# A recurrent mixer's TensorE order written by a planner in the source, small matmuls in runs, and a norm factor moved behind the projection

## The chip, the core and the metric

The kernel runs on one NeuronCore of one Trainium2 chip. The metric is the device time of one execution in microseconds (us). Every engine of the core (TensorE, VectorE, ScalarE, GpSimd, and SyncE, whose queue issues most of the DMAs) works through its own instructions in order and waits on semaphores for the others. In the profile TensorE's matmuls are called PE and its weight loads PEld, VectorE is DVE, ScalarE is ACT, GpSimd is POOL, SyncE is SP.

## What is computed

A decoder trunk of two layers on a sequence of 1024 tokens of width 1024, float32. The first layer's mixer has eight retention heads and eight RWKV-7 heads side by side; the second layer's is a sliding-window attention. Each is followed by a SwiGLU feed-forward block (FFN). Cut to what the change touches:

```python
n = rms_norm(h, norm1_g[0])            # x * rsqrt(mean(x^2) + eps) * g
z = n @ w_in                           # 1024 x 3840: q,k,v,g of retention; r,k,v,w,a,g of RWKV
q = rotary(q); k = rotary(k) / 8
o = chunk_retention(q, k, v)           # chunks of 128, state carried from chunk to chunk
ret_out = head_group_norm(o) * silu(g)
zs = z_rwkv + mu * (token_shift(z_rwkv) - z_rwkv)
...                                    # decay, gate and removal key from small low-rank projections
y = rwkv7_scan(r, decay, k, v, -kk, kk * a)   # delta rule, one state of 64 x 64 for each head
rwkv_out = (head_group_norm(y) + bonus) * gate
h = h + concat(ret_out, rwkv_out) @ w_out
h = h + swiglu(rms_norm(h, norm2_g[0]))       # and so on: attention, a second FFN, a last norm
```

## The kernel before, in words

Everything is stored transposed: features on the 128 partitions, tokens along the free axis, in two halves of 512 tokens (`hf` 0 and 1). A weight is read as tiles of 128 output features by 1024 inputs. `wload` loads one (512 KB) through SP's queue into one of two raw buffers `wr`, ScalarE rounds it to fp32r (`wh`, L163), and GpSimd subtracts to get the rest (`wl`, L164). `gemm` (L172 to L174) then issues 24 fp32r matmuls of 128x512 for the tile: for each of the eight input blocks high by high, high by low, low by high, all into one PSUM tile `ps_f`, of which there are three. All other matmuls of the mixer are plain float32 and small; each stands in the trace as two records, a transpose as one.

`mixer0` handles one half after the other. `norm` loads the half's eight x tiles, squares them on ScalarE (L188), adds them on VectorE (L193), sums over the partitions with a matmul against a constant (L195), turns that into the factor r = rsqrt(mean + eps) (L197, L198), loads x again, multiplies x by gain and r (L208) and splits the product (L178, L180) into the normalised input `nT` of all projections. So no projection starts before the factor is known.

The heads are worked in pairs `p` = 0 to 3 (two heads fill 128 partitions), the pairs of RWKV in units of two pairs. For one pair `rw_proj` makes three projections through `shifted` (a `gemm`, a copy of PSUM to `z` by ScalarE at L338, the token shift), and `rw_a1` makes decays, keys and the tiles `AR`, `BK`, `UV` (with small matmuls at L380, L388, L397, L423 and transposes at L432). For a unit, `rw_a2` makes the 64x64 products inside chunks, `GG` (L476), with transposes and identity matmuls (L488, L494, L500). `rw_inv` inverts triangular 32x32 blocks on VectorE: `GG` goes to DRAM (`dn`) and back as `DT`, 31 steps of two instructions follow (L530, L534), and the result goes out (`dg`) and back as `GT`. `rw_w` combines the blocks (L557 to L604), `rw_chain` carries the state through eight chunks (matmul L625, VectorE L631, one after the other), and `rw_y` makes the output in the one PSUM tile `ps_y`: for each chunk and head a 64x64 matmul with the state (L648) and an accumulating one with 128 rows (L649) alternate. Norm, bonus and gate follow (L652 to L661), and the result goes to DRAM (`cats`).

`ret` does one retention pair: four projections with rotary parts on SP's DMA queue, transposes, scores (L760: four chunks of one head, then four of the other), the state, and the output, in which a 128-row matmul with a block-diagonal state tile `Sb` (L772) and two others (L774) alternate into one PSUM tile. After both halves, `wout` multiplies the concatenated outputs with `w_out` (eight `gemm`s for each half; its addition on VectorE is L321), and the FFN follows.

The program is written with a tile framework. It allocates the buffers, places the semaphores, and its scheduler decides the order of each engine's instructions ahead of time from its own estimates. In the kernel before, that order is what TensorE runs: the scheduler mixes single matmuls of the projections with small matmuls, one by one. TensorE then takes them in that order, whatever is late.

Of the kernel before, what the change touches and what calls it, by code (L numbers as in the profile page):

```python
# [101 lines left out]

class Kern:
    def __init__(self, ctx, tc, A, out):
# [3 lines left out]
        self.ps = ctx.enter_context(tc.tile_pool(name="ps", bufs=1, space=bass.MemoryType.PSUM))  # L108
# [9 lines left out]
        self.cats = [self.dram(f"cat{hf}", [KT, P, HT]) for hf in range(2)]  # L118

# [19 lines left out]

    def s8(self, pool, tag, n, dt=F32):  # L140

        return [self.t(pool, [P, 4, HT], tag, n, dt) for _ in range(n)]

    def pst(self, tag, shape):
        return self.t(self.ps, shape, "ps_" + tag, {"f": 3, "m": 2, "r": 1, "c": 1, "y": 1}[tag])
# [6 lines left out]
    def wload(self, ap, width=1024):  # L152

        nc = self.nc
        raw = self.t(self.pp, [P, 1024], "wr", 2)
        nc.sync.dma_start(raw[:, :width], ap)
# [9 lines left out]
        return res  # L166

# [33 lines left out]
    def norm(self, h, g, s8):  # L201

# [3 lines left out]
        for k in range(KT):  # L206
            n = self.t(self.pp, [P, HT], "nq", 4)
            nc.vector.scalar_tensor_tensor(  # L208
                out=n, in0=h(k), scalar=self.col(g, k), in1=r, op0=ALU.mult, op1=ALU.mult
            )  # L210
            a, b = s8[k // 4][:, k % 4, :], s8[2 + k // 4][:, k % 4, :]
            self.split(n, a, b, k % 2 == 0)
            res.append((a, b))
# [15 lines left out]
    def mixer0(self):  # L229
# [25 lines left out]
        self.wa, self.gl, self.nT, self.cs = [None, None], [None, None], [None, None], [None, None]  # L255
        proj, st = {}, {}

        def pj(hf, p):
            proj[hf, p] = self.rw_proj(hf, p)

        def a1(hf, p):
            st[hf, p] = self.rw_a1(hf, p, proj.pop((hf, p)))

        def unit(hf, pairs):
            ss = [st.pop((hf, p)) for p in pairs]
            for p, x in zip(pairs, ss):
                self.rw_a2(x)
            self.rw_inv(ss)
            for x in ss:
                self.rw_w(x)  # L270
            self.rw_chain(hf, pairs, ss)
            for p, x in zip(pairs, ss):
                self.rw_y(hf, p, x)

        for hf in range(2):

            def x(k):
                t = self.t(self.pp, [P, HT], "nq", 4)
                nc.sync.dma_start(t, self.A["xT"][k, :, hf * HT : (hf + 1) * HT])
                return t  # L280

            self.nT[hf] = self.norm(x, "n1a", self.s8(self.pp, "s8", 4, F32R))
            self.ropes(hf)
            self.lora(hf)
            pj(hf, 0)
            a1(hf, 0)
            pj(hf, 1)
            a1(hf, 1)
            unit(hf, (0, 1))
            self.ret(hf, 0)  # L290
            pj(hf, 2)
            a1(hf, 2)
            self.ret(hf, 1)
            pj(hf, 3)
            a1(hf, 3)
            unit(hf, (2, 3))
            self.ret(hf, 2)
            self.ret(hf, 3)
        gr.__exit__(None, None, None)
        self.ghx, self.hx = self.pool("hx", "left")  # L300
        self.h[0] = self.wout(0, self.s8(self.pp, "s8", 4, F32R), self.s8(self.hx, "h0", 2))
        gm.__exit__(None, None, None)

    def wout(self, hf, ch8, h8):

        nc = self.nc
        hi, lo = ch8[0:2], ch8[2:4]
        ch = []
        for k in range(KT):
            c = self.t(self.pp, [P, HT], "nq", 4)  # L310
            nc.sync.dma_start(c, self.cats[hf][k])
            a, b = hi[k // 4][:, k % 4, :], lo[k // 4][:, k % 4, :]
# [11 lines left out]
    def ropes(self, hf):  # L324
        self.cs[hf] = (
            self.const(self.rp, "cos", (hf * HT, HT), eng=self.nc.sync),
            self.const(self.rp, "sin", (hf * HT, HT), eng=self.nc.sync),
        )

    def shifted(self, hf, ti, out):  # L330

        nc = self.nc
        w = self.wload(self.A["w_in"][16 + ti])
        ps = self.pst("f", [P, HT])
        self.gemm(ps, w, self.nT[hf])
        z = self.t(self.rp, [P, HT + 1], "z", 1)
        nc.gpsimd.tensor_copy(z[:, 0:1], self.zlast[:, ti : ti + 1])
        nc.scalar.copy(z[:, 1 : HT + 1], ps)  # L338
        nc.gpsimd.tensor_copy(self.zlast[:, ti : ti + 1], z[:, HT : HT + 1])
        nc.gpsimd.tensor_tensor(out=out, in0=z[:, 0:HT], in1=z[:, 1 : HT + 1], op=ALU.subtract)  # L340
        nc.vector.scalar_tensor_tensor(
            out=out, in0=out, scalar=self.col("mu", ti), in1=z[:, 1 : HT + 1], op0=ALU.mult, op1=ALU.add
        )

    def lora(self, hf):
        nc = self.nc
        wa = self.wa[hf] = self.t(self.mp, [P, HT], "wa", 1)
        gl = self.gl[hf] = self.t(self.mp, [P, HT], "gl", 2)
        self.shifted(hf, 12, wa)
        nc.scalar.activation(wa[0:64, :], wa[0:64, :], AF.Tanh)  # L350
        self.shifted(hf, 13, gl)
        nc.scalar.activation(gl, gl, AF.Tanh, scale=0.5)
        nc.vector.tensor_scalar(out=gl, in0=gl, scalar1=0.5, scalar2=0.5, op0=ALU.mult, op1=ALU.add)

    def rw_proj(self, hf, p):
        r = self.t(self.mp, [P, HT], "rr", 1)
        k = self.t(self.mp, [P, HT], "rkk", 1)
# [711 lines left out]
```

## Time and profile before

| | us |
|---|---|
| median of three runs | 2885.43 (2883.05 to 2896.56) |
| the profiled execution, whole | 2885.72 |
| its span, first to last instruction | 2883.9 |
| first matmul of a projection starts | 38.3 |
| last output of the RWKV heads is finished (end of L661, start of the last one 867.1) | 868 |
| last addition of the output projection (L321) starts | 965.4 |
| TensorE busy over the span | 2626.0 (91%) |
| VectorE, ScalarE, GpSimd busy | 1038.0, 1019.7, 1314.8 |

The change lies in the first 966 us. A busy time is the time in which at least one such instruction was under way, so divided by the count it gives the spacing of records that follow one another closely, while the mean duration of one includes its way through the array. A row of the waits says which instruction TensorE stood before, and what came last of that which it waited for. The granted clock is the share of full speed that the throttle let TensorE have.

### The profile page before, as it was taken

Reading aid. Unit: us, or ns where it says so; the run is one execution under the profiler, and the core shown is the slowest. Engines: PE = TensorE matmul, PEld = TensorE weight load, DVE = VectorE, ACT = ScalarE, POOL = GpSimd, SP = SyncE. Lnnn points to the kernel's source line nnn. Section 1 sums busy time; section 2 is a strip of 40 time slices with the busy share of each in tenths; the row PEclk is TensorE's granted clock in tenths of the full one; section 3 lists DMA queues with packets and bytes.
Section 4 is the critical chain, followed back from the end, with each engine's and each line's share of the span. In section 5 each row is a group of like instructions: output and inputs, shape, how many; then the busy total and the mean of one; then the engine's idle time right before and its main releaser. Section 6 shows DMA issues by size and latency. Waiting matters only on the chain. (4 is left out here: it accounts for less than half of the span.)

```text
span 2883.9 us, 35835 instructions
## 1 busy us (share of the span) xinstructions
PE 2626.0 (91%) x13484; PEld 2049.2 (71%) x13484; DVE 1038.0 (36%) x1810; ACT 1019.7 (35%) x1865; POOL 1314.8 (46%) x1140
## 2 busy tenths in 40 slices
PE   4799987888898899998999999989999999899997
PEld 2576664666676778886867888867678888688876
DVE  2554553554652421123193111333831112511113
ACT  3424323424343432223353222344533223422223
POOL 3533323433434555554424555544145555555553
PEclk9898998998998999998999999999999999999999
DMA  4221222121224222323302232432022223322332
GB/s 132 91 69 46 68 63 90 55 69 43 69 78 152 68 95 93 96 95 118 116 30 74 95 95 89 131 112 78 29 77 95 91 89 105 102 95 92 95 98 81
DMA packets 122908, 249.64 MB, mean 87 GB/s; under 512 B 37744, under 2 KB 48624, under 8 KB 122736
## 3 DMA queue, kind: packets, MB, share of 16 engines
q1 hardware_dynamic: 116480, 237.68, 25.8%
q10 hardware_dynamic: 6256, 9.67, 1.0%
q8 instruction: 107, 1.75, 0.2%
q14 instruction: 65, 0.53, 0.1%
HBM read 227.25 MB, written 14.68 MB: 84 GB/s over the span
## 5 line engine op out<-in xcount | busy, mean ns | idle before, releaser
L164 POOL TENSOR_TENSOR wl<-wr,wh 128x512 fp32r<-128x512 f32 (+1 forms) x776 | 997.1, 1287 | 1223.0 <-ACT wh L163 1146.0
L172 PE MATMUL ps_f<-s,wh 128*128 128x512 f32 x2336 | 939.6, 404 | 37.5 <-ACT s L178 27.2
L173 PE MATMUL ps_f<-s,wh 128*128 128x512 f32 x2336 | 938.9, 402 | 15.3 <-POOL s L180 12.0
L174 PE MATMUL ps_f<-s,wl 128*128 128x512 f32 x2336 | 940.9, 403 | 2.1 <-POOL wl L164 2.1
L163 ACT CAST wh<-wr 128x512 fp32r<-128x512 f32 (+1 forms) x776 | 472.3, 611 | 1316.3 <-PE ps_f L173 1086.8
L172 PEld LDWEIGHTS ps_f<-s,wh 128*128 128x128 f32 x2336 | 449.9, 193 | 152.8 <-ACT s L178 33.9
L173 PEld LDWEIGHTS ps_f<-s,wh 128*128 128x128 f32 x2336 | 449.5, 192 | 124.1 <-POOL s L180 17.8
L174 PEld LDWEIGHTS ps_f<-s,wl 128*128 128x128 f32 x2336 | 450.7, 193 | 107.4 <-issue 10.1
L173 PE MATMUL ps_f<-hl,wh 128*128 128x512 f32 x704 | 278.7, 396 | 18.8 <-POOL hl L180 18.8
L172 PE MATMUL ps_f<-hh,wh 128*128 128x512 f32 x704 | 275.7, 393 | 9.3 <-DVE h L819 7.4
L174 PE MATMUL ps_f<-hh,wl 128*128 128x512 f32 x704 | 274.5, 392 | 0.0
L819 DVE SCALAR_TENSOR_TENSOR h<-ps_f,h 128x512 f32<-128x512 f32 x192 | 132.5, 690 | 341.8 <-PE ps_f L174 341.8
L802 DVE SCALAR_TENSOR_TENSOR sl<-sl,ps_f 128x512 f32<-128x512 f32 x88 | 60.4, 687 | 437.2 <-ACT sl L801 437.2
L173 PEld LDWEIGHTS ps_f<-hl,wh 128*128 128x128 f32 x704 | 133.1, 189 | 55.4 <-POOL hl L180 28.5
L806 DVE TENSOR_TENSOR sl<-sl,ps_f 128x512 f32<-128x512 f32 x88 | 60.5, 687 | 289.0 <-PE ps_f L174 288.9
L172 PEld LDWEIGHTS ps_f<-hh,wh 128*128 128x128 f32 x704 | 133.0, 189 | 40.1 <-ACT nq L188 7.8
L174 PEld LDWEIGHTS ps_f<-hh,wl 128*128 128x128 f32 x704 | 133.1, 189 | 27.2 <-issue 0.2
L180 POOL TENSOR_TENSOR hl<-sl,hh 128x512 fp32r<-128x512 f32 x88 | 113.9, 1295 | 20.4 <-ACT hh L178 20.4
L180 POOL TENSOR_TENSOR s<-nq,s 128x512 fp32r<-128x512 f32 x40 | 63.8, 1604 | 77.5 <-ACT s L178 77.5
L193 DVE TENSOR_TENSOR nq<-nq,nq 128x512 f32<-128x512 f32 x70 | 59.8, 854 | 44.1 <-ACT nq L188 41.7
L178 ACT CAST s<-nq 128x512 fp32r<-128x512 f32 x80 | 48.3, 618 | 64.0 <-DVE nq L208 51.4
L909 ACT ACTIVATE s<-s,st 128x256 f32<-128x256 f32 (+1 forms) x128 | 62.0, 486 | 18.4 <-DVE st L906 18.4
(224 smaller groups left out, 2299.8 us busy)
## 6 DMA issues: line engine op xcount, KB each, us to landing
wr<-in_w_gate SPq DMA_DIRECT2D x88, 512.0 KB, 3.2
wr<-in_w_up SPq DMA_DIRECT2D x88, 512.0 KB, 3.3
wr<-in_w_down SPq DMA_DIRECT2D x128, 256.0 KB, 2.6
wr<-in_w_in SPq DMA_DIRECT2D x60, 512.0 KB, 3.3
wr<-in_w_down SPq DMA_DIRECT2D x64, 192.0 KB, 2.3
wr<-in_w_qkv SPq DMA_DIRECT2D x24, 512.0 KB, 3.2
nq<-in_xT SPq DMA_DIRECT2D x32, 256.0 KB, 2.7
wr<-in_w_out SPq DMA_DIRECT2D x16, 512.0 KB, 3.2
```

The costliest lines, as they stand in the source:

```text
L163: nc.scalar.copy(hi[:, :n], raw[:, c])
L164: nc.gpsimd.tensor_tensor(out=lo[:, :n], in0=raw[:, c], in1=hi.bitcast(F32)[:, :n], op=ALU.subtract)
L172: nc.tensor.matmul(ps, hi, rh, start=k == 0, stop=False)
L173: nc.tensor.matmul(ps, hi, rl, start=False, stop=False)
L174: nc.tensor.matmul(ps, lo, rh, start=False, stop=k == n - 1)
L178: nc.scalar.copy(hi, src)
L180: e.tensor_tensor(out=lo, in0=src, in1=hi.bitcast(F32), op=ALU.subtract)
L193: nc.vector.tensor_tensor(out=acc, in0=acc, in1=sq, op=ALU.add)
L802: V.scalar_tensor_tensor(out=sl, in0=sl, scalar=1.0, in1=pg, op0=ALU.add, op1=ALU.mult)
L806: V.tensor_tensor(out=sl, in0=sl, in1=pu, op=ALU.mult)
L819: V.scalar_tensor_tensor(out=hk, in0=ps, scalar=0.5, in1=hk, op0=ALU.mult, op1=ALU.add)
L909: S.activation(s[:, h, kw], s[:, h, kw], AF.Exp, bias=m[:, h : h + 1], accum_out=den[:, h : h + 1])
```

## The change

Three things change in the first mixer. First, TensorE's order is written out when the program is built: the parts of the mixer are generators that yield what they need next and how long to wait for it, and a class `Plan` runs them against an estimated clock `now`, which each matmul advances by an estimate. Whenever no generator is due, `Plan.step` issues the next three matmuls of the current projection. Each matmul is passed to `keep_in_program_order`, so that the framework's scheduler no longer moves it on TensorE; the other engines are scheduled as before. The projections are jobs in one fixed list. The units are chained: from the second one on, a unit's pair makes `GG` only after the unit ahead has made its output (`y{u-1}`), while its keys and decays are made earlier, for which `rr`, `rkk`, `rv`, `BK` get two buffers and `AR` four.

Second, small matmuls are regrouped: those of `GG` and of the retention scores alternate between the two heads (upper and lower 64 rows) with two PSUM tiles, and the two parts of an output that alternated in one PSUM tile are now made one after the other in two PSUM tiles, which ScalarE and VectorE add. `Sb` is gone: the state part uses two 64-row matmuls.

Third, `nT` is x times the gain alone (`gained`); the factor r is multiplied into the projections' results when they leave PSUM: on VectorE for RWKV, v and g (in place of ScalarE's copies), and through cos and sin for q and k. The first half's x is loaded once and its squares are summed by eight matmuls between those of the first projection; the second half's squares are summed on GpSimd while the first half is worked.

The `s8` tiles of four blocks become `n8` tiles of two blocks, in the whole kernel, and the first mixer has its own PSUM pool (three `f`, four `m`, one `c`).

```diff
+class Plan:
+    def step(self):
+        c = self.cur
+        if c is None:
+            if not self.jobs:
+                return None
+            t = self.time(self.jobs[0]["need"], 0.0)
+            if t is None or t > self.now:
+                return t
+            self.prefetch()
+            c = self.cur = self.jobs.popleft()
+            self.prefetch()
+            c["ps"], c["k"], c["rhs"] = self.K.pst("f", [P, HT]), 0, c["rhs"]()
+        ...
+        (hi, lo), (rh, rl) = c["hl"][k], c["rhs"][k]
+        self.K.mm(c["ps"], hi, rh, start=k == 0, stop=False)
+        self.K.mm(c["ps"], hi, rl, start=False, stop=False)
+        self.K.mm(c["ps"], lo, rh, start=False, stop=k == n - 1)
+        ...
+    def run(self):
+        while self.gens or self.jobs or self.cur:
+            nxt = []
+            for g in self.gens:
+                t = self.time(g[1], g[2])
+                if t is not None and t <= self.now:
+                    try:
+                        need, d = next(g[0])
+                        g[1], g[2] = need, self.now + d
+                    except StopIteration:
+                        self.gens.remove(g)
+                    break
+                ...
+            else:
+                t = self.step()
+                ...
+    def mm(self, out, lhsT, rhs, **kw):
+        i = self.nc.tensor.matmul(out, lhsT, rhs, **kw)
+        self.tc.keep_in_program_order(i)
+        ...
+        if rhs.dtype == F32R:
+            self.plan.now += 0.000443 * n
+        else:
+            self.plan.now += max(0.05, 0.00167 * n * (0.6 if lhsT.shape[0] <= 64 or lhsT.shape[1] <= 64 else 1.0))
 def mixer0(self):
+        pl.chain(self.first_norm(x0))
+        for u, (hf, p0) in enumerate(units):
+            pl.chain(self.unit(u, hf, (p0, p0 + 1)))
+        for u, (hf, p0) in enumerate(units):
+            for p in (p0, p0 + 1):
+                pl.chain(self.pair(u, hf, p))
+        for hf in range(2):
+            for p in range(4):
+                pl.chain(self.ret(hf, p))
+        pl.chain(self.second_norm())
+        self.lora(0)
+        jobs(0, "rkv", (0, 1))
+        jobs(0, "ret", (0, 1))
+        jobs(0, "rkv", (2, 3))
+        jobs(0, "ret", (2, 3))
+        self.lora(1)
+        jobs(1, "rkv", (0, 1))
+        jobs(1, "ret", (0,))
+        jobs(1, "rkv", (2, 3))
+        jobs(1, "ret", (1, 2, 3))
+        pl.run()
+    def gained(self, x, g, n8, k):
+        self.nc.scalar.activation(a, x, AF.Copy, scale=gc)
+        self.nc.vector.scalar_tensor_tensor(
+            out=b, in0=x, scalar=gc, in1=a.bitcast(F32), op0=ALU.mult, op1=ALU.subtract
+        )
+    def first_norm(self, x0):
+        for k in range(KT):
+            self.nT.append(self.gained(x0[k], "n1a", n8, k))
+            nc.scalar.activation(sq, x0[k], AF.Square)
+            ...
+            self.mm(ps, self.cst["ones"], sq, start=k == 0, stop=k == KT - 1)
 shifted:
-        nc.scalar.copy(z[:, 1 : HT + 1], ps)
+            nc.vector.tensor_tensor(out=z[:, 1 : HT + 1], in0=ps, in1=self.rs, op=ALU.mult)
 pair (was rw_a1 and rw_a2):
+        yield (), 6.0        # after the two low-rank matmuls
+        ...
+        yield ((f"r{hf}_{p}", 5.0), (f"v{hf}_{p}", 5.0)), 8.0
+        ...
+        yield (), 12.0
+        if u:
+            yield ((f"y{u - 1}", 1.0),), 0.0
+        for h in range(2):
+            pss = [self.pst("m", [P, 4, P]) for _ in range(2)]
+            for i in range(4):
+                for e in range(2):
+                    self.mm(pss[e][:, i, :], BK[half[e], c, ...], AR[half[e], c, :], start=True, stop=True)
 unit (was rw_inv, rw_w, rw_chain and rw_y):
+        yield tuple((f"n{u}_{p}", 3.5) for p in pairs), 0.0
+        ...                  # DT loads, then 31 steps, after each second one:
+            if j % 2:
+                yield (), 2.4
+        ...                  # dg stored, GT loaded
+        yield tuple((f"a{u}_{p}", 1.0) for p in pairs), 7.0
+        ...
+        for c in range(NCH): # the state
+            ...
+            yield (), 1.3
+            y1, y2 = self.pst("m", [P, NCH, 64]), self.pst("m", [P, NCH, 64])
+            for c in range(NCH):
+                for e, a in enumerate(half):
+                    self.mm(y1[a, c, :], UV[:, c, e, :], GG[:, c, e, 64:P], start=True, stop=True)
+            for c in range(NCH):
+                for a in half:
+                    self.mm(y2[a, c, :], GT[a, c, :], AR[a, c, 64:P], start=True, stop=True)
+            S.copy(y, y1.rearrange("p c t -> p (c t)"))
+            V.tensor_tensor(out=y, in0=y2.rearrange("p c t -> p (c t)"), in1=y, op=ALU.add)
 ret:
+            for e, a in enumerate(half):
+                self.mm(pss[e][:, c, :], k[a, tk], q[a, tk], start=True, stop=True)
+        ...
+        for c in range(4):
+            for e, a in enumerate(half):
+                self.mm(p1[a, c, :], vt[:, c, e, :], sc[e][:, c, :], start=True, stop=True)
+        for c in range(4):
+            for a in half:
+                self.mm(p2[a, c, :], Sc[a, c, :], qd[a, c, :], start=True, stop=True)
```

## The prediction

> **What bounds the kernel now.** I read the page first, then busy time and granted clock by stretch, TensorE's waits in the mixer, and its groups of small matmuls.
>
> ```profile
> span 2883.9 us, 35835 instructions
> PE 2626.0 (91%) x13484; PEld 2049.2 (71%) x13484; DVE 1038.0 (36%) x1810; ACT 1019.7 (35%) x1865; POOL 1314.8 (46%) x1140
> ```
>
> ```profile
> core 0: us, PE busy (x) PEld busy (x) DVE busy (x) ACT busy (x) POOL busy (x), PEclk, DMA share, GB/s
> 0.00:38.30 38.30, 2.11 (x3) 0.54 (x3) 7.04 (x13) 12.89 (x18) 7.50 (x16) 1.00 0.55 172
> 38.30:867.00 828.70, 716.30 (x5048) 528.05 (x5048) 433.25 (x791) 300.28 (x489) 323.77 (x356) 0.89 0.22 68
> 867.00:966.00 99.00, 88.90 (x373) 70.88 (x372) 23.27 (x31) 31.47 (x51) 43.68 (x34) 0.90 0.40 137
> 1031.00:2883.00 1852.00, 1764.57 (x7853) 1408.32 (x7852) 535.35 (x935) 639.08 (x1251) 896.68 (x707) 0.98 0.28 91
> ```
>
> TensorE bounds everything after 1031 us. The first 966 us are another matter: its busy time is 2.1 + 716.3 + 88.9 = 807.3, so it stands idle for 158.7 us: 36.2 before the first projection, 112.4 in the mixer, 10.1 in the output projection. VectorE is busy for 433 of 829 us there, so no other engine is the limit; what is lost is waits, slow small matmuls and clock. The change touches nothing after 966 us but the size of buffers, which I cost at nothing: the same matmuls at 95% busy cover it.
>
> ```profile
> engine line waited for: us in total, times, longest us
> PE ps_m L423 <- DVE rr L421: 40.4, 8, 6.7
> PE ps_m L195 <- DVE nq L193: 32.0, 1, 32.0
> PE ps_m L397 <- ACT rt L395: 20.2, 5, 7.5
> PE ps_f L172 <- ACT s L178: 11.6, 2, 7.4
> PE ps_c L563 <- DVE TZ L557: 8.1, 3, 3.4
> ```
>
> ```profile
> 0.00:867.00 867.00, 76.09 (x496) 53.02 (x496) 6.01 (x8) 4.78 (x8) 0.90 0.24 73
> ...
> 0.00:867.00 867.00, 413.25 (x1478) 289.15 (x1478) 5.43 (x8) 34.76 (x60) 0.90 0.24 73
> ...
> 1100.00:1300.00 200.00, 197.65 (x870) 162.64 (x869) 35.88 (x52) 6.51 (x11) 1.00 0.30 96
> ...
> 432.00:504.00 72.00, 53.26 (x193) 35.38 (x192) 25.20 (x26) 28.38 (x42) 27.13 (x31) 0.81 0.27 90
> ```
>
> The first row is `ps_y` alone: 153 ns a record. The second is `ps_f`: a projection's matmul takes 279.6 ns in the mixer, against 227.2 ns in the FFN (third row, at full clock). The fourth is a stretch of the mixer with 19 us of idle TensorE and a clock of 0.81.
>
> **The change part by part.** I sum the first 966 us, TensorE's busy time first.
>
> ```profile
> L476 PE MATMUL ps_m<-AR,BK 64*128 64x128 f32 x256 | 29.7, 284 | 0.7 <-DVE GG L480 0.2
> L760 PE MATMUL ps_r<-r,r 64*128 64x128 f32 x128 | 25.8, 356 | 6.7 <-DVE Sret L744 6.3 <-DVE r L762 0.3
> L625 PE MATMUL ps_c<-S,M 64*64 64x64 f32 x240 | 15.8, 229 | 0.0
> L595 PE MATMUL ps_m<-GG,W 64*64 64x128 f32 x256 | 15.7, 272 | 0.0
> L774 PE MATMUL ps_r<-r,r 128*64 128x128 f32 x112 | 13.1, 314 | 0.0
> L772 PE MATMUL ps_r<-r,r 128*128 128x128 f32 x50 | 12.9, 344 | 0.6 <-DVE r L762 0.6
> L604 PE MATMUL ps_m<-UV,GG 128*64 128x64 f32 x256 | 9.2, 225 | 0.5 <-DVE AR L600 0.3
> L494 PE MATMUL ps_m<-c_ident,AR 64*64 64x64 f32 x256 | 9.2, 221 | 0.0
> L782 PE MATMUL ps_m<-r,c_blk 128*128 128x512 f32 x16 | 8.7, 625 | 0.7 <-ACT r L780 0.7
> ```
>
> RWKV output. `y1` is 256 records of exactly L604's form, `y2` 256 of L494's, both in runs: 9.2 + 9.2 = 18.4 for 76.1, so -57.7. At L625's price `y2` is 16.9 and the gain 50.
>
> `GG`. In L476 four matmuls in a row use the same 64 rows, 116 ns a record. Now the halves alternate, as in L595 (61 ns, also 128 tokens): 15.7 for 29.7, -14.0. If two outputs of 128 columns don't overlap: 0. I take L595, the nearest row with alternating halves.
>
> Scores. 128 records at 61 ns are 7.8 for 25.8: -18.0; at L476's price, 14.8: -11.0.
>
> Retention output. L772 and L774, whole, are 12.9 x 56/50 + 13.1 x 128/112 = 29.4 (the window cuts the last pair). The new 256 records are 64-wide over 128 tokens, in runs: 15.7, so -13.7; at worst 0.
>
> Norm. Nine sums of squares for two, each 8.7/8 = 1.09: +7.6.
>
> Projections. The surplus is 1478 x (279.6 - 227.2) = 77 us. Part of it is splitting: a change of tile form costs 153 - 36 = 117 ns by the `ps_y` row. In the built order of instructions the tile form changes 510 times up to the last RWKV output before and 302 times after; 219 of the 510 are `ps_y`'s own, so elsewhere it is 291 against 302. Some 291 x 0.117 = 34 us stay; the other 43 are clock. I take -25, because the longest waits go, with 0 and -77 as ends.
>
> On this splitting the Trainium skill ("TensorEngine Tiling", Key Properties) says that changing the tiling mode, not just the tile, drains TensorE. The 153 against 36 ns agree with it, and it speaks against issuing projections in threes between small runs: by it alone the projections gain nothing.
>
> Busy: 807.3 - 57.7 - 14.0 - 18.0 - 13.7 + 7.6 - 25 = 686.5. Ends: 754 (gains of 50, 0, 11, 0, 0) and 634.
>
> Now idle time.
>
> ```profile
> wr<-in_w_in SPq DMA_DIRECT2D x60, 512.0 KB, 3.3
> nq<-in_xT SPq DMA_DIRECT2D x32, 256.0 KB, 2.7
> L163 ACT CAST wh<-wr 128x512 fp32r<-128x512 f32 (+1 forms) x776 | 472.3, 611 | 1316.3 <-PE ps_f L173 1086.8
> L164 POOL TENSOR_TENSOR wl<-wr,wh 128x512 fp32r<-128x512 f32 (+1 forms) x776 | 997.1, 1287 | 1223.0 <-ACT wh L163 1146.0
> ```
>
> Start. The first projection needs no factor. SP's queue holds eight x tiles ahead of the first weight: 8 x 0.26 + 0.52 = 2.6 MB, at the 172 GB/s of the first row 15 us, and 0.6 + 1.3 for the split with its hand-overs make 18 instead of 36. Eight x loads fewer in all; at a DMA share of 0.22 the rest of the DMAs are covered by compute.
>
> Long waits. The matmul of L397 was ordered too close behind ScalarE, that of L423 too close behind VectorE. The plan puts 6.0 us ahead of the first and at least 8.0 + 12.0 ahead of the second: -60.6. Late next is the inverse:
>
> ```profile
> L476 PE MATMUL ps_m<-AR,BK x64: 271/272/374, 333.7 to 344.9; 64*128 64x128 f32 x64
> L530 DVE TENSOR_TENSOR xt<-X,DT x31: 181/272/1378, 353.1 to 382.5; 128x126 f32<-128x126 f32 x3, 128x30 f32<-128x30 f32 x2, 128x56 f32<-128x56 f32 x2, 128x78 f32<-128x78 f32 x2
> L557 DVE STREAM_TRANSPOSE TZ<-GT x4: 432/434/436, 388.8 to 393.2; 32x256 f32<-32x256 f32 x4
> L625 PE MATMUL ps_c<-S,M x56: 216/218/267, 402.6 to 417.7; 64*64 64x64 f32 x56
> ```
>
> This is unit two. The 31 steps take 382.5 - 353.1 = 29.4 us, the plan allows 15 x 2.4 = 36; from the last step to L557 6.3, the plan 7.0. Only the state's step is tight: 15.1/7 = 2.16 us here, with output matmuls between, against 1.3 and its own matmuls (0.25) in the plan: up to 32 x 0.6 = 19 us, which I leave to the range, since those output matmuls (8 x 0.153 a step) explain it. For new waits at the fixed places I take 15; ends 0, and 61 + 19, as much as goes.
>
> Idle: 18 + (112.4 - 60.6) + 15 + 10 = 95.
>
> VectorE. 44 results leave PSUM there instead of through ScalarE:
>
> ```profile
> L424 DVE TENSOR_TENSOR bv<-rv,ps_m 128x512 f32<-128x512 f32 x8 | 5.5, 685 | 7.4 <-PE ps_m L423 7.4
> L338 ACT COPY z<-ps_f 128x512 f32<-128x512 f32 x28 | 16.3, 581 | 19.5 <-DVE rr L341 11.9 <-DVE rkk L341 3.8 <-PE ps_f L174 3.2
> L208 DVE SCALAR_TENSOR_TENSOR nq<-nq,pv,nq 128x512 f32<-128x512 f32 x15 | 14.3, 956 | 20.2 <-DMA nq<-in_xT 16.6 <-ACT nq L198 3.3
> ```
>
> With 16 sums of two PSUM tiles that is 60 x 0.685 = 41 us; `gained` and L208 cancel (16 of each), and the squares' sums leave. 433 becomes about 460, some 60% of the shorter stretch: costed at nothing, covered by TensorE. GpSimd takes seven sums and four products with cos and sin, about 15 us on 324, off the path.
>
> Sum: 686.5 + 95 = 781.5 for 966.0, so -184.5. The profiled execution took 2885.7 (span 2883.9 and 1.8 around it), 0.3 above the median of the runs: 2885.7 - 184.5 = 2701, forecast 2700. With the ends: 634 + 80 (no new wait) gives 2634; 754 + 160 gives 2834.
>
> **The rivals.** Waits change places. Order fixed on TensorE means that whatever is late on VectorE stops everything behind it, and the order before was static too and had 158.7 us of waits. Idle as before: +64, 2765. Against it: the plan's leads are longer than the rows above.
>
> The drain decides: the clock doesn't recover, the projections stay at 279.6 ns: +25, 2725.
>
> The clock recovers wholly: 227.2 ns, 2648. For it: 0.81 goes with 19 us idle, 1.00 with 2. The Trainium skill ("TensorE: Matmul & The Clock Gate", Part 1) says that an idle window of about 3.4 us halves the clock until a busy window has passed; the trace's stretches agree.
>
> Slower: the units' latency becomes the bound.
>
> ```profile
> L476 PE MATMUL ps_m<-AR,BK x256: 271/272/374, 145.2 to 763.1; 64*128 64x128 f32 x128
> ```
>
> Each unit now waits for the output of the one ahead, and VectorE, with the PSUM results in its queue, does the inverse between them. From L476 to the end of L625 is 84 us above, so about 90 with the output. Unit one's `GG` starts at about 125 (145.2 before, less 18): 125 + 4 x 90 + 70 for the last output projection is 555, hidden under 781. It shows from (781 - 195)/4 = 147 us a unit and makes the kernel slower from 193, 2.1 times what is measured; at 205 it is 2935. What could do it is SP's queue: weight loads stand behind the store `dg` that waits for the inverse, and two buffers cover 2 x 24 x 0.227 = 11 us.
>
> **How the numbers follow.** Forecast about 2700 (2665 to 2715): 0.42. Clock recovers, 2648: 0.16. Drain decides, 2725: 0.16. Waits change places, 2765, up to 2834 with its ends: 0.15. Slower: 0.08. The planned order brings nothing: 0.03. The range 2615 to 2825 leaves out the last two and the far ends. 0.5% (14 us) is about what can be told from no change; faster 0.89, same 0.03, slower 0.08.
>
> **What would show it.** Right: `y1` and `y2` at about 40 ns a record; `GG` near 60; the first projection near 18 us; the wait before the matmuls of `rr` and `rt` with `c_blk` gone; `ps_f` at 240 to 270 ns; output projection done near 780. Wrong: TensorE waiting for the state's steps, for GT, or for weight splits over many us in each unit, or VectorE over 80% busy in the mixer.

## The result, and the profile after

The changed kernel takes 2738.95 us (median; 2735.00 to 2743.06) where the kernel before takes 2885.33 (2883.05 to 2896.56): 0.9485 of the time, with a 95% interval of 0.9456 to 0.9515. The forecast was 2700, its range 2615 to 2825. The direction and the place were right, 146 us went where 185 were forecast, and one term of the sum is the chief reason.

The page of the changed kernel begins so (span, then busy time, share of the span and instructions of each engine):

```profile
span 2741.2 us, 36080 instructions
PE 2539.6 (93%) x13602; PEld 1983.9 (72%) x13602; DVE 1046.2 (38%) x1846; ACT 1017.0 (37%) x1861; POOL 1315.1 (48%) x1125
```

Busy time and granted clock of the changed kernel by stretch; `a:b`, its length, then busy us and instructions of each engine, the clock, the DMA share and GB/s:

```profile
core 0: us, PE busy (x) PEld busy (x) DVE busy (x) ACT busy (x) POOL busy (x), PEclk, DMA share, GB/s
0.00:827.10 827.10, 722.17 (x5540) 536.46 (x5540) 472.14 (x870) 342.64 (x554) 373.95 (x390) 0.92 0.30 90
0.00:16.70 16.70, 2.09 (x3) 0.52 (x3) 1.07 (x4) 3.21 (x5) 2.74 (x14) 1.00 0.88 279
16.70:766.00 749.30, 658.99 (x5271) 485.97 (x5272) 450.06 (x842) 318.14 (x514) 334.22 (x349) 0.91 0.28 80
766.00:827.10 61.10, 61.10 (x269) 49.97 (x267) 21.02 (x25) 21.28 (x36) 36.99 (x28) 1.00 0.47 158
888.00:2740.00 1852.00, 1764.79 (x7858) 1407.64 (x7858) 536.13 (x936) 639.53 (x1252) 899.30 (x708) 0.98 0.29 91
```

The output projection ends at 827 us instead of 966, and that is nearly the whole gain: the profiled executions differ by 2885.7 - 2743.1 = 142.6, the stretch by 139. The last 1852 us are the same to 0.3 us of TensorE. In the stretch TensorE's busy time fell from 807.3 to 722.2, its idle time from 158.7 to 827.1 - 722.2 = 104.9. VectorE is busy for 450 of 749 us of the mixer, 60%.

TensorE's longest waits in the first 850 us of the changed kernel (total, times, longest):

```profile
engine line waited for: us in total, times, longest us
PE ps_m L209 <- ACT nq L452: 14.1, 2, 13.2
PE ps_m L220 <- DVE r L883: 13.8, 3, 8.3
PE ps_m L220 <- DVE GG L631: 9.0, 1, 9.0
PE ps_c L209 <- DVE GT L821: 8.4, 3, 3.9
PE ps_f L209 <- POOL wl L278: 8.3, 5, 2.0
PE ps_f L209 <- ACT wh L277: 8.1, 5, 3.6
```

Before, two lines held 40.4 and 20.2 us and the start 32.0; now no line holds more than 14.1, and most rows of the whole list are one or two events. The first is still the start: 13.2 of its 14.1 us lie before TensorE's first matmul. `L883` is v's result leaving VectorE ahead of v's transposes, `L631` the mask on `GG`, `L821` the state's step.

The groups of small matmuls that the change regrouped, in the changed kernel (busy us and mean ns of one, then idle time before them; `L209` is the helper through which every matmul goes):

```profile
L209 PE MATMUL ps_m<-AR,BK 64*128 64x128 f32 x256 | 23.6, 315 | 5.8 <-DVE rt L856 3.8 <-ACT rt L850 1.3 <-DVE bv L616 0.4
...
L209 PE MATMUL ps_m<-nq,c_ones 128*128 128x512 f32 x18 | 12.0, 754 | 14.1 <-ACT nq L452 14.1
...
L209 PE MATMUL ps_m<-r,r 128*64 128x128 f32 x128 | 11.2, 316 | 1.4 <-DVE r L939 1.4
...
L209 PE MATMUL ps_m<-r,Sc 64*64 64x128 f32 x128 | 10.4, 301 | 0.0
...
L209 PE MATMUL ps_m<-wa,wua 64*128 64x512 f32 x32 | 10.1, 640 | 0.7 <-DVE UV L784 0.7
...
L209 PE MATMUL ps_m<-r,r 64*128 64x128 f32 x128 | 9.3, 283 | 3.8 <-issue 3.8
L209 PE MATMUL ps_m<-GG,UV 128*64 128x64 f32 x256 | 9.2, 225 | 0.0
L209 PE MATMUL ps_m<-AR,GT 64*64 64x64 f32 x256 | 9.2, 221 | 0.0
```

The last two rows are the RWKV output, 18.4 us in place of 76.1. `AR,BK` is `GG` (29.7 before), `r,r 64*128` the scores (25.8), `r,r 128*64` with `r,Sc` the retention output. The low-rank matmuls `wa,wua` took 9.0 and 8.9 us in two groups before, which is 17.9, and now 10.1.

The projections of the whole stretch (the tile `ps_f` alone), first before, then after:

```profile
0.00:966.00 966.00, 496.38 (x1824) 356.46 (x1824) 16.20 (x24) 34.76 (x60) 0.90 0.25 79
```

```profile
0.00:827.10 827.10, 492.45 (x1824) 350.69 (x1824) 41.09 (x60) 9.25 (x16) 0.92 0.30 90
```

The same 1824 records, and only 3.9 us less.

### The profile page after: what moved, and what is told of

Read it like the earlier page. It is cut to its first block, busy times and chain, and to the rows that moved or that the text cites. A ratio compares the mean times of both kernels' runs of the same rounds, so it can differ in the third digit from the quotient of the medians.

```text
span 2741.2 us, 36080 instructions
## 1 busy us (share of the span) xinstructions
PE 2539.6 (93%) x13602; PEld 1983.9 (72%) x13602; DVE 1046.2 (38%) x1846; ACT 1017.0 (37%) x1861; POOL 1315.1 (48%) x1125
## 5 line engine op out<-in xcount | busy, mean ns | idle before, releaser
L290 PE MATMUL ps_f<-n,wh 128*128 128x512 f32 x1856 | 734.0, 396 | 15.7 <-ACT n L296 15.7
L291 PE MATMUL ps_f<-n,wh 128*128 128x512 f32 x1856 | 734.4, 396 | 4.5 <-POOL n L298 2.8
L292 PE MATMUL ps_f<-n,wl 128*128 128x512 f32 x1856 | 732.4, 395 | 0.5 <-POOL wl L278 0.4
L290 PEld LDWEIGHTS ps_f<-n,wh 128*128 128x128 f32 x1856 | 352.2, 190 | 97.6 <-ACT n L296 19.1
L291 PEld LDWEIGHTS ps_f<-n,wh 128*128 128x128 f32 x1856 | 352.3, 190 | 85.8 <-issue 5.6
L292 PEld LDWEIGHTS ps_f<-n,wl 128*128 128x128 f32 x1856 | 352.3, 190 | 80.2 <-issue 6.0
L209 PE MATMUL ps_f<-n,wh 128*128 128x512 f32 x960 | 335.6, 432 | 11.0 <-ACT wh L277 8.1
L209 PEld LDWEIGHTS ps_f<-n,wh 128*128 128x128 f32 x960 | 182.9, 200 | 69.8 <-issue 17.1
L1001 DVE SCALAR_TENSOR_TENSOR sl<-sl,ps_f 128x512 f32<-128x512 f32 x88 | 60.4, 687 | 437.1 <-ACT sl L1000 437.1
L209 PE MATMUL ps_f<-n,wl 128*128 128x512 f32 x480 | 198.5, 414 | 8.5 <-POOL wl L278 8.3
L1005 DVE TENSOR_TENSOR sl<-sl,ps_f 128x512 f32<-128x512 f32 x88 | 60.4, 686 | 287.9 <-PE ps_f L292 287.8
L209 PEld LDWEIGHTS ps_f<-n,wl 128*128 128x128 f32 x480 | 96.1, 200 | 33.6 <-POOL wl L278 11.8
```

The costliest lines, as they stand in the source:

```text
L209: i = self.nc.tensor.matmul(out, lhsT, rhs, **kw)
L290: nc.tensor.matmul(ps, hi, rh, start=k == 0, stop=False)
L291: nc.tensor.matmul(ps, hi, rl, start=False, stop=False)
L292: nc.tensor.matmul(ps, lo, rh, start=False, stop=k == n - 1)
L1001: V.scalar_tensor_tensor(out=sl, in0=sl, scalar=1.0, in1=pg, op0=ALU.add, op1=ALU.mult)
L1005: V.tensor_tensor(out=sl, in0=sl, in1=pu, op=ALU.mult)
```

## The experiments

Three questions were open after the first look. How much is the regrouping and how much the order? What holds the projections at 270 ns a record (492.45 us for 1824; 272 before, 227.2 in the FFN), the pieces in which they are issued or the clock? And are the remaining waits worth anything? Every run is compared with the kernel before on the same chip. "End" is the end of the output projection, "idle" is that end less TensorE's busy time, and "half" is the time up to that end in which the trace's records of the granted clock say 0.50, added up.

| run | us | of before, 95% interval | end | idle | half |
|---|---|---|---|---|---|
| before | 2885.33 | 1 | 966 | 159 | 195 |
| after | 2738.95 | 0.9485 (0.9456 to 0.9515) | 827 | 105 | 130 |
| e1 scheduler's order | 2726.14 | 0.9443 (0.9413 to 0.9472) | 811 | 90 | 109 |
| e2 RWKV output alternates | 2815.93 | 0.9757 (0.9723 to 0.9792) | 900 | 104 | 198 |
| e3 leads halved | 2769.94 | 0.9601 (0.9570 to 0.9632) | 854 | 139 | 133 |
| e4 leads times 1.25 | 2732.17 | 0.9467 (0.9439 to 0.9495) | 819 | 104 | 109 |
| e5 heads in turn | 2732.38 | 0.9460 (0.9438 to 0.9483) | 817 | 90 | 106 |
| e6 start held back | 2724.98 | 0.9440 (0.9412 to 0.9467) | 806 | 95 | 106 |
| e7 no leads, scheduler alone | 2839.17 | 0.9831 (0.9807 to 0.9855) | 928 | 191 | 212 |
| e8 before, output in runs | 2826.50 | 0.9785 (0.9757 to 0.9812) | 905 | 161 | 137 |
| e9 six leads lengthened | 2720.12 | 0.9417 (0.9397 to 0.9438) | 805 | 100 | 85 |
| e10 e9 + e1 + e6 | 2711.39 | 0.9386 (0.9361 to 0.9411) | 794 | 93 | 68 |
| e11 e8 with two tiles | 2827.40 | 0.9793 (0.9767 to 0.9819) | 909 | 162 | 140 |
| e12 pieces of 12 | 2720.08 | 0.9418 (0.9397 to 0.9439) | 803 | 104 | 85 |

**The RWKV output alone, put back and taken alone.** In e2 the changed kernel's two kinds of output matmuls alternate one by one again, still into two tiles:

```diff
             for c in range(NCH):
                 for e, a in enumerate(half):
+                    self.mm(y2[a, c, :], GT[a, c, :], AR[a, c, 64:P], start=True, stop=True)
                     self.mm(y1[a, c, :], UV[:, c, e, :], GG[:, c, e, 64:P], start=True, stop=True)
-            for c in range(NCH):
-                for a in half:
-                    self.mm(y2[a, c, :], GT[a, c, :], AR[a, c, 64:P], start=True, stop=True)
```

> The changed kernel, but in the RWKV output the 64-row and 128-row matmuls alternate again, one by one, still into two PSUM tiles and at the same place of the plan. If each change of tile form costs the 117 ns read from the kernel before and TensorE's time bounds this stretch: the 512 records take about 78 us instead of 18, and the time is 2785 to 2800. Rival, that the runs lie in time in which TensorE would wait anyway: 2739 to 2755.

It took 2815.93 us, 77 more than the changed kernel and 16 more than I expected at most. The stretch and the two groups in e2:

```profile
core 0: us, PE busy (x) PEld busy (x) DVE busy (x) ACT busy (x) POOL busy (x), PEclk, DMA share, GB/s
0.00:900.10 900.10, 796.54 (x5540) 584.57 (x5540) 472.59 (x870) 344.46 (x554) 371.79 (x390) 0.89 0.27 83
```

```profile
L209 PE MATMUL ps_m<-GG,UV 128*64 128x64 f32 x256 | 55.7, 316 | 0.0
L209 PE MATMUL ps_m<-AR,GT 64*64 64x64 f32 x256 | 55.4, 312 | 0.0
```

The same 5540 records keep TensorE busy for 74 us longer (796.5 against 722.2; the two groups overlap), idle time is as it was, and the half-clock time rises from 130 to 198 us. By the trace's records the two groups together are under way for 93 us, and 76 of these lie at half clock.

In e8 the kernel before makes its output in two runs, 128-row matmuls first and 64-row ones behind, in its one tile; the counts and shapes are those of before, but the RWKV output of e8 is not the reference's (the tile seems not to keep the sum of both parts), so e8 counts for its time alone. In e11 the two runs go to two tiles, which ScalarE and VectorE add:

```diff
-        yps = self.pst("y", [P, HT])
+        y1, y2 = self.pst("y", [P, HT]), self.pst("c", [P, HT])
+        c0 = 1 if hf == 0 else 0
...
-                if not first:
-                    nc.tensor.matmul(yps[a, tk], St[a, c, :], AR[a, c, 64:P], start=True, stop=False)
-                nc.tensor.matmul(yps[a, tk], UV[:, c, e, :], GG[:, c, e, 64:P], start=first, stop=True)
+                nc.tensor.matmul(y1[a, tk], UV[:, c, e, :], GG[:, c, e, 64:P], start=True, stop=True)
+        for c in range(c0, NCH):
+            tk = slice(64 * c, 64 * c + 64)
+            for a in half:
+                nc.tensor.matmul(y2[a, tk], St[a, c, :], AR[a, c, 64:P], start=True, stop=True)
+        yy = self.t(mp, [P, HT], "rt", 6)
+        S.copy(yy, y1)
+        V.tensor_tensor(out=yy[:, 64 * c0 :], in0=y2[:, 64 * c0 :], in1=yy[:, 64 * c0 :], op=ALU.add)
```

> The kernel before with one edit: in the RWKV output the 128-row matmuls of all chunks come first and the 64-row ones after them, into the same PSUM tile. If the alternation alone, with the clock that it holds down, is worth 77 us: 2805 to 2830. Rival, that in this kernel the alternating matmuls lie in time in which TensorE waits for the chunk states anyway: 2860 to 2885.

> The kernel before, its RWKV output made in two runs into two PSUM tiles (the second is the one of the state's steps), added by ScalarE and VectorE as in the changed kernel. If the alternation of tile forms is worth as much here as where it was put back: 2805 to 2830, as with one PSUM tile. Rival, that the shared PSUM tile and eight more additions on VectorE eat it: 2850 to 2885.

They took 2826.50 and 2827.40 us, 60 us less than the kernel before each time. The stretch in e11:

```profile
core 0: us, PE busy (x) PEld busy (x) DVE busy (x) ACT busy (x) POOL busy (x), PEclk, DMA share, GB/s
0.00:909.00 909.00, 746.93 (x5422) 560.12 (x5422) 469.64 (x842) 349.34 (x566) 376.21 (x405) 0.92 0.28 84
```

Busy time falls by 60.4 (807.3 to 746.9) and idle time stays (159 before, 162 here). So this one regrouping, some twenty lines, is 60 of the 146 us when done alone and 77 when taken out of the rest. That the second part goes through two more instructions per pair costs nothing that shows (e8 against e11). TensorE's two long waits are still there in e11 (first view below), and yet its half-clock time falls from 195 to 140 us, and the projections take 487.57 us (second view) where they took 496.38:

```profile
PE ps_m L423 <- DVE rr L421: 30.9, 8, 5.7
PE ps_m L397 <- ACT rt L395: 21.6, 5, 7.6
```

```profile
0.00:909.00 909.00, 487.57 (x1824) 352.13 (x1824) 16.25 (x24) 34.81 (x60) 0.92 0.28 84
```

**The order, in its two halves.** The change fixes TensorE's order, and it writes the program in that order. In e1 only the first goes: the two calls of `keep_in_program_order` are removed and the scheduler may move matmuls again.

```diff
     def mm(self, out, lhsT, rhs, **kw):
         i = self.nc.tensor.matmul(out, lhsT, rhs, **kw)
-        self.tc.keep_in_program_order(i)
```

> The changed kernel, but TensorE's instructions are no longer held in the planner's order: the framework's scheduler orders them again. Regrouping, norm and buffers stay. If the planner's order is what removed the waits: idle TensorE in the output-projection stretch goes from 106 us back to some 150, the scheduler again mixes single projection matmuls with small ones, and the time is 2790 to 2840. Rival, that regrouping and the early start did it and the order nothing: 2739 +- 15.

2726.14 us: not slower, and its interval overlaps that of the changed kernel. Fixing the order brings nothing by itself. The scheduler keeps it nearly as it is written: the tile form changes 318 times in the built order up to the last RWKV output, 302 with the order fixed.

In e7 the plan's leads go as well (each is multiplied by 0, so a part follows as soon as what it needs has been issued); the regrouping, the norm factor and the buffers stay. In e3 the leads are halved and the order stays fixed, in e4 they are a quarter longer. In e3 and e7 the retention's last step waits by name for the gate, which the leads no longer ensure.

```diff
-                        g[1], g[2] = need, self.now + d
+                        g[1], g[2] = tuple((n, 0.5 * x) for n, x in need), self.now + 0.5 * d
```

> The changed kernel with all lead times zero and TensorE's order left to the framework's scheduler: the program is then written part by part, each as soon as its inputs are written, and only the scheduler mixes projections with the rest. Regrouping, norm and buffers stay. If the plan's clock is what fills the waits, by the order in which the program is written: idle TensorE 150 us or more and 2790 to 2830. Rival, that regrouping, early start and earlier keys of the next unit make the gain: 2725 to 2750.

> The changed kernel, but the plan reckons with half of every lead time (the retention's last step then waits for its gate by name). If the leads are what keeps TensorE from standing before late data: idle TensorE in the first 828 us goes from 106 to 160 or more, more half-clock time with it, and the time is 2790 to 2850. Rival, that TensorE's work alone sets the time: 2739 +- 15.

> The changed kernel, but the plan reckons with 1.25 times every lead time. If the waits that are left (single ones of 2 to 9 us) come from leads that are too short: idle falls from 106 to 70 or 80 us, half-clock time from 140 to about 100 us, the projections go below 270 ns a record, and the time is 2700 to 2720. Rival, that the units' latency is close to the bound: longer leads lengthen each unit, 2740 to 2770.

They took 2839.17, 2769.94 and 2732.17 us. TensorE's longest waits in e7, then in e3:

```profile
engine line waited for: us in total, times, longest us
PE ps_c L209 <- DVE X L744: 53.4, 11, 19.8
PE ps_m L209 <- DVE rr L606: 46.8, 8, 6.5
PE ps_m L209 <- ACT rt L567: 20.7, 6, 8.5
```

```profile
engine line waited for: us in total, times, longest us
PE ps_m L209 <- DVE rr L608: 35.1, 6, 12.8
PE ps_c L209 <- DVE X L746: 30.4, 14, 10.3
```

`rr` and `rt` are the two waits that the forecast removed (`L423` and `L397` before, 40.4 and 20.2 us), and without leads they come back with 46.8 and 20.7; `X` is the inverse, which is the wait that was named as late next. The leads are worth 113 us (e7 against e1), not through any one matmul but through where the program puts the projections between the small ones. That is measured against this program without leads, not against the order of the kernel before: e11, with that order and the regrouped output, is 88 us above the changed kernel, and those 88 hold everything else that the change does. A quarter more brings nothing that can be told apart. e7 is 12 us slower than e11, though it contains what e11 does; which of its other parts costs that was not tried.

**Heads in turn, and the start.** e5 puts back four matmuls of one head and then four of the other in `GG` and the scores; e6 lets the projections start only once the norm's factor is there.

```diff
-            for i in range(4):
-                for e in range(2):
+            for e in range(2):
+                for i in range(4):
```

```diff
-            if k == 0:
-                self.plan.done("n0")
-                yield (), 0.0
...
+        self.plan.done("n0")
```

> The changed kernel, but GG and the retention scores again do four matmuls of one head and then four of the other. If alternating heads overlap in the array: GG goes from 23.6 us of TensorE back to about 30, the scores from 9.3 to about 15 to 25, and the time is 2750 to 2765. Rival, that this is hidden under waits: 2739 to 2745.

> The changed kernel, but the first projection is planned only after the first half's norm factor is there, as before; x is still loaded once. If the early start is worth its time: first projection near 30 us instead of 16.7, and 2750 to 2757. Rival, that the first unit's latency sets this stretch and the projections catch up: 2739 to 2745.

2732.38 and 2724.98 us: neither is slower than the changed kernel, where I expected 11 to 26 us more of e5 and 11 to 18 of e6. The edit of e5 is shown for `GG`; that of the scores is alike. The two groups of e5:

```profile
L209 PE MATMUL ps_m<-AR,BK 64*128 64x128 f32 x256 | 32.4, 310 | 3.4 <-DVE GG L631 2.2 <-ACT rt L850 1.3
...
L209 PE MATMUL ps_m<-r,r 64*128 64x128 f32 x128 | 15.0, 304 | 4.7 <-DVE r L876 4.7
```

They take 32.4 + 15.0 against 23.6 + 9.3, so alternating does save 14.5 us of busy time there; but the end comes 10.6 us sooner in e5, with less idle time (90 us against 105) and less half-clock time (106 against 130); which edit of the order moved which wait was not traced. In e6 the first projection starts at 21.4 instead of 16.7, and the end comes 22 us sooner, again with 106 us at half clock. e1, e4, e5 and e6 are four small disturbances of the plan, and all end 7 to 14 us below the unchanged plan: the changed kernel's own schedule looks like an unlucky one among its neighbours, and a part worth less than that can't be read from one such pair.

**The waits that are left.** e9 lengthens six leads, ahead of matmuls that the waits above name; in the order of the diff: after each half of `GG`, before `UV` is used, after the copy of `TZ`, at each step of the state, before the output's norm, and between v and its transposes:

```diff
-            yield (), 0.6
+            yield (), 2.0
-        yield (), 5.0
+        yield (), 9.0
-        yield (), 2.5
+        yield (), 3.5
-            yield (), 1.3
+            yield (), 1.7
-        yield (), 3.0
+        yield (), 5.0
-        yield ((f"retk{hf}_{p}", 9.0), (f"retv{hf}_{p}", 1.5)), 0.0
+        yield ((f"retk{hf}_{p}", 9.0), (f"retv{hf}_{p}", 7.0)), 0.0
```

> The changed kernel with six lead times lengthened where TensorE still waited: 7.0 for the retention's v (1.5 before), 2.0 after each half of GG (0.6), 9.0 ahead of UV's use (5.0), 1.7 for a step of the state (1.3), 3.5 after the copy of the inverse's part (2.5), 5.0 ahead of the output's norm (3.0). If those waits are what is left: idle TensorE from 106 to 80 us, half-clock time from 140 to about 100 us, 2700 to 2715. Rival, that a lead taken longer at one place moves the wait to another: 2725 to 2740, like 1.25 times every lead.

2720.12 us, outside the interval of the changed kernel and 5 us above what I expected at most. Idle time fell by only 5 us, half-clock time by 45. In e10 the edits of e9, e1 and e6 stand together:

> The targeted leads, TensorE's order by the scheduler, and the first projection held until the factor is there. Each of the last two alone measured some 13 us faster than the changed kernel. If these differences are effects of their own, they add: 2685 to 2705. Rival, that each is only another way for the same waits to fall out: 2715 to 2730.

2711.39 us, the fastest, with 0.9386 of the time before and 1% below the changed kernel. It is 6 us above the 2685 to 2705 that I expected: the gains of the three don't add up. The stretch in e10:

```profile
core 0: us, PE busy (x) PEld busy (x) DVE busy (x) ACT busy (x) POOL busy (x), PEclk, DMA share, GB/s
0.00:794.20 794.20, 701.69 (x5540) 523.16 (x5540) 471.26 (x870) 340.51 (x554) 367.13 (x390) 0.96 0.31 94
```

Against the changed kernel, idle time is 12 us lower and busy time 20.5 lower with the same 5540 records, at a clock of 0.96 instead of 0.92.

**The pieces of a projection.** In e12 a projection goes on by 12 matmuls at a time instead of 3 once its inputs are whole, and the scheduler is free as in e1, so e1 is what it stands against:

```diff
-        (hi, lo), (rh, rl) = c["hl"][k], c["rhs"][k]
...
-        c["k"] += 1
+        m = 4 if len(c["rhs"]) == n and k % 4 == 0 else 1
+        for k in range(k, k + m):
+            (hi, lo), (rh, rl) = c["hl"][k], c["rhs"][k]
...
+        c["k"] += m
```

> The changed kernel with projections planned in pieces of twelve matmuls and not three, TensorE's order by the scheduler (to compare with the run that changes the order alone, 2726): a projection is left for something else 112 times and not 147. If leaving and coming back costs some 0.2 to 0.3 us each: projections fall from 277 to about 271 ns a record, but the state's steps wait longer behind each piece; TensorE-bound 2715 to 2722. Rival, that the pieces lengthen each unit by 8 x 2 us and more: 2740 to 2790.

2720.08 us, 6 less than e1. The projections (`ps_f` alone) up to the end of the output projection in e1, e12, e10 and e7, as shown above for before and after:

```profile
0.00:810.80 810.80, 490.66 (x1824) 347.11 (x1824) 41.06 (x60) 9.26 (x16) 0.93 0.30 92
...
0.00:803.20 803.20, 475.21 (x1824) 346.36 (x1824) 41.09 (x60) 9.24 (x16) 0.95 0.31 93
...
0.00:794.20 794.20, 475.41 (x1824) 340.02 (x1824) 40.92 (x60) 9.26 (x16) 0.96 0.31 94
...
0.00:927.60 927.60, 459.78 (x1824) 350.14 (x1824) 40.99 (x60) 9.22 (x16) 0.89 0.25 80
```

The records are the same 1824 each time. Two things can be counted for them in the traces: how often a projection is left for other matmuls, and how much of the time in which a projection's matmul is under way lies at half clock.

| run | projections, busy us | of it at half clock, us | times left |
|---|---|---|---|
| before | 496.4 | 71 | 130 |
| after | 492.5 | 59 | 142 |
| e1 | 490.7 | 49 | 148 |
| e12 | 475.2 | 35 | 113 |
| e10 | 475.4 | 27 | 137 |
| e7 | 459.8 | 36 | 77 |

e12 and e10 come out alike, one with 24 pieces fewer, the other with 8 us less at half clock. A least-squares fit over all fourteen kernels gives 420 us, and 0.53 us for each at half clock, and 0.30 us for each time that a projection is left; it misses none by more than about 4 us; at the FFN's 227.2 ns the 1824 records would take 414. So by this estimate the changed kernel's projections carry some 31 us of clock and 43 of pieces. The split is not firm: e7 has by far the fewest pieces, and without it a piece comes to 0.18 us. e7 also shows that the clock of a whole stretch says little of one group: its mean, 0.89, is the lowest of the four, yet only 36 of its 212 us at half clock lie on projections.

## Why the prediction came out as it did

- **RWKV output, -57.7: exact.** 9.2 + 9.2 us at 36 ns a record, as read from the rows `L604` and `L494`. Its whole effect was underrated, though: put back it costs 77. The 153 ns of the alternating records, and with it the 117 for a change of tile form, held clock too: 26.5 of the 76.1 us lay at half clock before, and 76 of the 93 in e2.
- **`GG`, -14.0: -6.1.** 92 ns a record, where `L595`'s 61 was taken and 116 would have been no gain. By the trace's records 6.7 of the 23.6 us lie at half clock, where before none did; between records that follow one another at full clock it is 65 ns, near `L595`'s 55, so the overlap was read about rightly; what else `GG` lost was not traced. Against e5 the alternating heads save 8.8 us.
- **Scores, -18.0: -16.5. Retention output, -13.7: -9.6** (15.9 + 15.3 before over the whole stretch, 11.2 + 10.4 after). Ones matmuls, +7.6: +8.9 (3.1 for the mixer's two sums, 12.0 for its nine).
- **Projections, -25: -3.9. This is the term that failed.** Its step said that 43 of the surplus are clock and that 25 of them come back because the longest waits go. The waits went, and half-clock time in the stretch fell by 65 us. But only 12 of these lay on projections (71 us before, 59 after); on the small matmuls it fell from 99 to 46, where 26.5 had lain on the alternating outputs. Nor did the clock hang on those waits: in e11 they stay, and half-clock time falls by 55 us by the regrouping alone. By the fit, 12 us less at half clock give 6, and 12 pieces more take 4 back. I had counted changes of tile form over all small matmuls (291 against 302), which doesn't tell how often a projection is left (130 against 142). The rival "the drain decides" (2725) was nearest to the time, and its condition held: on the projections the clock hardly recovered, and the pieces stayed. The Trainium skill ("TensorEngine Tiling", Key Properties) says that changing the mode drains TensorE; e7 and e12 agree, with fewer pieces and faster projections than e1, though both also have less half-clock time there. It gives no price for a change.
- **Busy time: 686.5 forecast, 722.2 measured.** The terms that I had costed come to -84.9 by these rows, and the total fell by 85.1; groups overlap, so this is a rough book. What I had not costed cancels: the low-rank matmuls got 7.8 us cheaper, probably because the calls on the two row halves now follow each other, and others dearer.
- **Idle: 95 forecast, 104.9 measured, with luck.** The two long waits went, and e7 shows by their return that the leads had removed them (e3 shows it for `rr`). But the mixer keeps 90.3 us where 52 + 15 = 67 were forecast: if the 52 stayed, new waits took 38, not 15. What hides it is the output projection, with none of the 10 us left, and the start, 14.6 where 18 were taken. The first projection begins at 16.7, near the 18 forecast; but in e6, without the early start, it begins at 21.4, and e6 is no slower: 17 of the 22 us gained there come from the rest of the new norm.
- **VectorE, about 460 and 60%, costed at nothing:** 450 in the mixer and 60%. The units' latency as the bound (the slower rival) did not show: the last RWKV output is done at 765.
- **After 966, costed at nothing:** 3.7 us less, of 1919.7.
- **"Order fixed on TensorE":** the order as such was not what helps (e1); the leads by which the program is written are (e7, 113 us). The rival "the planned order brings nothing" falls by this.

What stays open: the cost of the norm factor and the buffers by themselves, the planner's order against the old one with all else equal, and whether shorter leads in one place with longer ones in another would leave the projections whole without new waits.

## What to carry to other kernels

Before planning an order, look for two small matmul shapes that alternate one by one, for here a regrouping of some twenty lines gave 60 of 146 us without any planner. For a long matmul chain count two things on its own records: how often it is left for something else, and how much of it runs at half clock; the half-clock time of the whole stretch fell by a third here, and the chain gained almost nothing. And where the text order of a program decides where its pieces land, test that order and the constraint that holds it apart; the constraint was worth nothing, the leads that make the order 113 us.

## What was not expected of the hardware

The clock was at half rate in stretches in which TensorE never stood idle. In the kernel before, ahead of and in such a stretch, in which 40 of the 68 records are the alternating output matmuls of unit two:

```profile
core 0: us, PE busy (x) PEld busy (x) DVE busy (x) ACT busy (x) POOL busy (x), PEclk, DMA share, GB/s
419.00:426.30 7.30, 5.35 (x42) 3.03 (x42) 3.40 (x8) 3.80 (x4) 2.09 (x4) 1.00 0.06 17
426.30:443.40 17.10, 17.10 (x68) 10.82 (x66) 3.54 (x5) 4.48 (x5) 0.23 (x1) 0.50 0.06 20
```

e2 shows it again with the alternation put back (90 of 96 and 98 of 106 records), each time with the 3.4 us ahead:

```profile
263.50:266.90 3.40, 3.40 (x29) 2.53 (x28) 0.82 (x2) 0.00 (x0) 1.25 (x1) 1.00 0.02 6
266.90:287.40 20.50, 20.50 (x96) 14.74 (x96) 1.38 (x2) 2.44 (x4) 1.06 (x2) 0.50 0.00 1
434.10:437.50 3.40, 3.40 (x28) 2.52 (x28) 0.75 (x1) 0.00 (x0) 0.63 (x2) 1.00 0.45 154
437.50:461.40 23.90, 23.90 (x106) 15.20 (x105) 2.11 (x4) 2.96 (x5) 1.06 (x2) 0.50 0.00 1
```

TensorE is busy for all of the 17.1, 20.5 and 23.9 us, at a clock of 0.50, and in e2 also for the 3.4 us before each. The Trainium skill ("TensorE: Matmul & The Clock Gate", Part 1) has the clock halved after an idle window of about 3.4 us and restored after a busy one. These rows do not agree with that, if busy is meant as the profile counts it; a matmul's modelled end may hide that the array itself had little to do, which no run here can tell. The prediction found the trace's stretches in agreement; the two that it shows, of 72 and 200 us, are too coarse to tell.

The changed kernel has 18 half-clock stretches of 3.4 to 13.7 us before its end, 15 of them behind 3.4 us with over 2 us of idle TensorE, so less than a whole idle window seems to be enough. In the table idle time alone explains the order of the runs badly (e4 and e12 both have 104 us, at 2732 and 2720). Half-clock time does better: 130, 109, 85 and 68 us go with 2739, 2726 (e1), 2720 (e9, e12) and 2711, about half a microsecond for each one at half rate. But it does not do it alone: e4 and e5 have 109 and 106 us at 2732, and e3 has 133, like the changed kernel, at 2770, with 139 us idle. It is a correlation over these variants, not a separate test of the clock.
